# Five instead of four 7-product row pairs in three column pairs of each MLP's first matrix, with the half-width weight blocks in buffers of their own

## The chip, the cores and the metric

The kernel runs on one core of a Trainium2 chip. The metric is the device time of one execution in microseconds (us). Below, TensorE is PE in the profile, VectorE is DVE, ScalarE is ACT, GpSimd is POOL, and SyncE, which issues the weight loads, is SP. A difference of less than 0.2%, some 5 us, is about what a measurement of this kernel cannot tell from no change.

## The reference

A two-layer decoder trunk on 256 tokens of width 2048, in float32: one retention layer with a squared-ReLU MLP, then one latent-attention layer with another such MLP. The change sits in the two MLPs, and the reference for them is short:

```python
def sq_relu_mlp(h, w1, w2):
    return jnp.square(jax.nn.relu(h @ w1)) @ w2
# in each of the two layers, with w1 (2048, 8192) and w2 (8192, 2048):
x = x + sq_relu_mlp(rms_norm(x, norm_mlp[layer]), mlp_w1[layer], mlp_w2[layer])
```

All other parts (the retention projections, the query, key and value projections, the softmax, the rotary tables) stay as they were, apart from where some constants and tables lie in the on-chip memory.

## The kernel before

**Three products for one.** TensorE multiplies operands in a rounded type, so the kernel writes each operand as a high part and a low part. A product of two blocks then takes three matmuls (lines 409 to 411): high by high, high by low, low by high. The high part of a weight block is a cast on ScalarE (line 216, tiles `wh`), the low part is a subtraction on VectorE (line 217, tiles `wl`).

**Quads.** In the MLPs the work comes in quads. A quad is one row pair (256 rows of a weight matrix) by one column pair (1024 columns), that is four weight blocks of 128 rows by 512 columns, loaded by one DMA of 1 MB into a tile `raw`. There are three `raw` buffers. Function `quad` (from line 321) multiplies a quad by the two token tiles in one of two ways:

- **8 products** (24 matmuls): the four blocks are split as they are. ScalarE makes two casts and VectorE two subtractions of 1024 columns.
- **7 products** (21 matmuls), after Strassen and Winograd: VectorE first makes sums of the weight blocks (line 363 with 1024 columns, lines 372 and 373 with 512 each), and then the blocks 11 and 22, the block 21 alone, and two pairs of sums are split. That is three splits of 1024 columns and one of 512, the **half block**. The activations need sums too; `with_sums` (line 451) makes them: three small operations on VectorE, one cast and one subtraction.

**Column pairs.** `gemm_pair` (line 386) runs eight quads, one after the other, over one column pair, and collects the products in PSUM tiles `c11` to `c22`, `p1`, `p5` and `p67`. Its list `kinds` says which row pairs take the 7-product way, so a list such as `SEVEN = (3, 5, 7)` names row pairs. At the end `pair_out` copies six results to SBUF on ScalarE (line 432) and joins them with four operations on VectorE (lines 434 to 439).

**The MLP.** `mlp` (line 864) takes the 8192 hidden columns in four groups of 2048. A group has four column pairs of eight quads each: two of the first matrix (named `u0_2` for layer 0, column pair 2; its quads are `u0_20` to `u0_27`), then two of the second matrix (`d0_10` and `d0_11` for group 1, whose quads are `d0_110` and so on). Column pairs 2, 4 and 6 are the first of the groups 2, 3 and 4. The results of the first matrix are joined (line 448, `summed`), multiplied and clipped on ScalarE (line 877), turned on TensorE (line 235, tiles `hid_tp`), squared and split. The results of the second matrix are added to `x` in device memory by accumulating DMAs from the POOL queue (line 152, tiles `xh`), except in the last group.

**What sets the order.** Every engine works through its own list in order. The lists are made when the program is built: the code issues parts, `later` delays a piece of work by so many quads, and a scheduler then orders each engine's list. At run time an engine waits at the head of its list until what it needs is there. Weight parts `wh` and `wl` have five buffers each. Before the change each of these has 1024 columns, and a half block occupies a whole one:

```python
wh = pool.tile([P, 1024], F32R, tag="wh", bufs=5, name=f"{name}_wh{part}")
wl = pool.tile([P, 1024], F32R, tag="wl", bufs=5, name=f"{name}_wl{part}")
```

A cast can therefore start only when the part five places before it has been multiplied. A new `raw` can be loaded when VectorE and ScalarE have read the quad three places before it.

Of the kernel before, what the change touches and what calls it, by code (L numbers as in the profile page):

```python
# [11 lines left out]
F32 = mybir.dt.float32  # L12
F32R = mybir.dt.float32r
# [3 lines left out]
ALU = mybir.AluOpType  # L17
# [18 lines left out]
P = 128  # L36
NT = 2
S = NT * P
# [7 lines left out]
GROUPS = (4, 4, 4, 4)  # L46
SEVEN, LATE, ODD, HEAD = (3, 5, 7), (5, 7), (1, 3, 5, 7), (2, 4, 6, 7)
QUERY, FOUR = (3, 4, 6, 7), (3, 5, 6, 7)
PI = math.pi

G_MIX0, G_MLP0, G_KV, G_MIX1, G_MLP1 = 0, 16, 32, 48, 64
G_CKV, G_CQ, G_KN, G_QN, G_ALL = 80, 84, 96, 97, 98
C_INVR, C_INVM, C_MASK, C_ID, C_ALL = 0, 128, 160, 544, 672

# [12 lines left out]
def yoco(ctx: ExitStack, tc: tile.TileContext, a):  # L67
    nc = tc.nc
# [6 lines left out]
    def small(w, name):  # L75
        return pool.tile([P, w], F32, tag="small", bufs=36, name=name)

# [19 lines left out]
    def later(n, fn):  # L97
        queue.append((clock[0] + n, next(count), fn))
# [16 lines left out]
    gains = pool.tile([P, G_ALL], F32, name="gains")  # L115
    cst = pool.tile([P, C_ALL], F32, name="cst")
    pos_i = pool.tile([P, NT], I32, name="pos_i")
    gpe = pool.tile([P, 2 * ROPE], F32, name="gpe")
    nc.scalar.dma_start(gains, a["gains"])
    ident = cst[:, C_ID : C_ID + P]  # L120
    mask = cst[:, C_MASK : C_MASK + 3 * P]
    neg_half = pool.tile([P, 16], F32, name="neg_half")
    nc.gpsimd.memset(neg_half, -0.5)
# [114 lines left out]
    def stream(w, chunk, cols, name, use, done=None, before=None):  # L238
# [5 lines left out]
        for half in range(2):  # L244
            wh = pool.tile([P, 1024], F32R, tag="wh", bufs=5, name=f"{name}_wh{half}")
            wl = pool.tile([P, 1024], F32R, tag="wl", bufs=5, name=f"{name}_wl{half}")
            cuts = 1
# [73 lines left out]
    def quad(w, chunk, x, mm, name, split_ends=False):  # L321
# [362 lines left out]
    def start(half):  # L684
        first_inputs(half)
        if half == 4:
            nc.sync.dma_start(pos_i, a["pos"])
            nc.sync.dma_start(cst, a["cst"])
            nc.sync.dma_start(gpe, a["gpe"])
        if half == 5:  # L690
            ret_tables()
        if half == 7:
            for b in range(NB):
                later(2 + b, lambda b=b: load_x(b))
            later(6, scale_tables)
            later(18, lambda: mla_sc.append(sincos(cst[:, C_INVM : C_INVM + 32], 32, "tm")))
            later(26, mla_tables)
# [166 lines left out]
    def mlp(layer, act, r, done):  # L864
        w1, w2 = a[f"mlp_w1_{layer}"], a[f"mlp_w2_{layer}"]
        f0 = 0
        for gi, nf in enumerate(GROUPS):
# [74 lines left out]
    rc, ckv = [], []  # L942
    kpe_t = pool.tile([P, 2, S], F32R, name="kpe_t")

# [167 lines left out]
    def score(b, qt, qpe):  # L1112
# [16 lines left out]
        for t in range(NT):  # L1129
            cols = slice(t * P, t * P + (t + 1) * P)  # L1130
            cut = mask[:, cols].unsqueeze(1).to_broadcast([P, 2, (t + 1) * P])
            nc.vector.tensor_tensor(p[t], sc[:, :, cols], cut, op=ALU.add)
# [82 lines left out]
def _constants():  # L1215
# [9 lines left out]
    causal = np.where(i[None, :] <= i[:, None], 0.0, -1e30)  # L1225
    cst[:, C_MASK : C_MASK + 3 * P] = np.concatenate([causal, np.zeros((P, P)), causal], axis=1)
    cst[:, C_ID : C_ID + P] = np.eye(P)
# [65 lines left out]
```

## Time and profile before

| what | value |
|---|---|
| median of 3 runs (lowest to highest) | 2459.8 us (2458.24 to 2460.84) |
| the profiled execution, its own time | 2458.1 us |
| its span, first to last instruction | 2456.3 us |
| TensorE busy | 2446.2 us, 11614 instructions |
| TensorE weight loads busy | 2057.6 us |
| VectorE busy | 2212.2 us, 2919 instructions |
| ScalarE busy | 1641.3 us |
| GpSimd busy | 238.0 us |
| DMA | 521.05 MB, mean 212 GB/s |

The busy share of TensorE counts matmuls that overlap, each with a modelled end, so it says that TensorE is nearly never idle and not how fast it is. The starts of its instructions tell the pace. VectorE's and ScalarE's idle time stands in the timeline in brackets ahead of what ended it. Outside the span lie 1.8 us of the profiled execution's time.

### The profile page before, as it was taken

What the parts mean: (1) busy time and instruction counts of PE and PEld (TensorE: products, weight loads), DVE (VectorE), ACT (ScalarE), POOL (GpSimd) and SP (SyncE); (2) the same over time, 40 slices, a digit from 0 to 9 for tenths busy, and PEclk for the clock granted to TensorE, in tenths of its full rate; (3) what the DMA queues carried; (4) which work ended last, traced back from release to release, by engine and by line L of the source; (5) the groups of instructions that cost most, each with busy time, mean ns of one, the idle gap of its engine ahead of it and who ended that gap; (6) DMA issues with size and microseconds to landing.
All of it is one profiled execution on the core that took longest, in us unless ns stands there. A gap on an engine that the chain in (4) does not pass through costs nothing.

```text
span 2456.3 us, 31721 instructions
## 1 busy us (share of the span) xinstructions
PE 2446.2 (100%) x11614; PEld 2057.6 (84%) x11614; DVE 2212.2 (90%) x2919; ACT 1641.3 (67%) x2307; POOL 238.0 (10%) x287
## 2 busy tenths in 40 slices
PE   9999999999999999999999999999999999999999
PEld 7888888888888888888888888998888888888887
DVE  7899899888899999999999998777899999999998
ACT  6566666556676767667676777577667667676674
POOL 6400001000000010010110001101000100100100
PEclk9999999999999999999999999999999999999999
DMA  8555569556565586695786555444555865957854
GB/s 309 207 201 191 192 202 259 191 183 224 197 218 194 196 254 218 207 272 187 241 253 213 200 202 180 155 162 173 197 199 205 252 228 194 262 198 229 264 209 170
DMA packets 93692, 521.05 MB, mean 212 GB/s; under 512 B 11104, under 2 KB 12512, under 8 KB 40288
## 3 DMA queue, kind: packets, MB, share of 16 engines
q1 hardware_dynamic: 72144, 472.83, 55.2%
q0 software_dynamic: 21248, 46.15, 8.9%
q8 instruction: 91, 1.49, 0.2%
q14 instruction: 65, 0.53, 0.1%
q10 hardware_dynamic: 144, 0.05, 0.0%
HBM read 479.14 MB, written 39.85 MB: 211 GB/s over the span
## 4 chain that ended last, share of the span: by engine, by line
PE 92%; DVE 2%; ACT 1%; issue 0%; DMA 0%; POOL 0%; ACTq 0%; DVEq 0%
PE u_c L411 7%; PE u_c L410 7%; PE u_c L409 7%; PE d_c L411 6%; PE d_c L410 6%; PE d_c L409 6%; PE rp_c L411 3%; PE rp_c L409 3%; PE rp_c L410 3%; PE u_p L411 2%; PE u_p L410 2%; PE u_p L409 2%; PE rq_acc L307 2%; PE rk_acc L307 2%; PE ro_c L411 2%; PE ro_c L409 2%
## 5 line engine op out<-in xcount | busy, mean ns | idle before, releaser
L217 DVE TENSOR_TENSOR d_wl<-d_raw,d_wh 128x1024 fp32r<-128x1024 f32 (+1 forms) x256 | 278.7, 1111 | 31.6 <-ACT d_wh L216 31.6
L217 DVE TENSOR_TENSOR u_wl<-u_raw,u_wh 128x1024 fp32r<-128x1024 f32 (+1 forms) x256 | 279.3, 1113 | 29.8 <-ACT u_wh L216 29.8
L409 PE MATMUL u_c<-u_wh,n 128*128 128x512 f32 x712 | 278.3, 392 | 0.0
L411 PE MATMUL u_c<-u_wh,n 128*128 128x512 f32 x712 | 277.2, 389 | 0.0
L410 PE MATMUL u_c<-u_wl,n 128*128 128x512 f32 x712 | 277.2, 389 | 0.0
L409 PE MATMUL d_c<-d_wh,hid 128*128 128x512 f32 x706 | 275.4, 392 | 0.5 <-ACT d_wh L216 0.5
L411 PE MATMUL d_c<-d_wh,hid 128*128 128x512 f32 x706 | 275.0, 390 | 0.0
L410 PE MATMUL d_c<-d_wl,hid 128*128 128x512 f32 x706 | 274.8, 389 | 0.0
L216 ACT CAST u_wh<-u_raw 128x1024 fp32r<-128x1024 f32 (+1 forms) x256 | 241.3, 973 | 49.6 <-PE u_c L411 24.1
L216 ACT CAST d_wh<-d_raw 128x1024 fp32r<-128x1024 f32 (+1 forms) x256 | 240.3, 971 | 39.9 <-PE d_c L411 16.6
L216 ACT CAST d_wh<-d_u 128x1024 fp32r<-128x1024 f32 x106 | 108.1, 1051 | 119.7 <-DVE d_u L373 82.6
L216 ACT CAST u_wh<-u_u 128x1024 fp32r<-128x1024 f32 x104 | 106.2, 1052 | 116.0 <-DVE u_u L373 77.3
L411 PEld LDWEIGHTS u_c<-u_wh,n 128*128 128x128 f32 x712 | 133.7, 188 | 27.8
L410 PEld LDWEIGHTS u_c<-u_wl,n 128*128 128x128 f32 x712 | 133.8, 188 | 27.4 <-DVE u_wl L217 0.3
L409 PEld LDWEIGHTS u_c<-u_wh,n 128*128 128x128 f32 x712 | 133.7, 188 | 27.0
L409 PEld LDWEIGHTS d_c<-d_wh,hid 128*128 128x128 f32 x706 | 132.6, 188 | 28.2 <-ACT d_wh L216 1.4
L411 PEld LDWEIGHTS d_c<-d_wh,hid 128*128 128x128 f32 x706 | 132.5, 188 | 27.6
L410 PEld LDWEIGHTS d_c<-d_wl,hid 128*128 128x128 f32 x706 | 132.6, 188 | 27.5 <-DVE d_wl L217 0.4
L216 ACT CAST rp_wh<-rp_raw 128x1024 fp32r<-128x1024 f32 x112 | 103.8, 945 | 74.2 <-PE rp_c L411 49.2
L217 DVE TENSOR_TENSOR rp_wl<-rp_raw,rp_wh 128x1024 fp32r<-128x1024 f32 x112 | 119.7, 1090 | 16.4 <-ACT rp_wh L216 16.2
L217 DVE TENSOR_TENSOR u_wl<-u_u,u_wh 128x1024 fp32r<-128x1024 f32 x104 | 123.5, 1222 | 3.1 <-ACT u_wh L216 2.8
L217 DVE TENSOR_TENSOR d_wl<-d_u,d_wh 128x1024 fp32r<-128x1024 f32 x106 | 125.8, 1221 | 0.0
(570 smaller groups left out, 6505.3 us busy)
## 6 DMA issues: line engine op xcount, KB each, us to landing
u_raw<-in_mlp_w SPq DMA_DIRECT2D x128, 1024.0 KB, 5.4
d_raw<-in_mlp_w SPq DMA_DIRECT2D x128, 1024.0 KB, 4.9
rp_raw<-in_ret_w_gv SPq DMA_DIRECT2D x56, 1024.0 KB, 4.8
ro_raw<-in_ret_w_out SPq DMA_DIRECT2D x32, 1024.0 KB, 4.9
uq_raw<-in_mla_w_uq SPq DMA_DIRECT2D x24, 768.0 KB, 4.3
rq_raw<-in_ret_w_qk SPq DMA_DIRECT2D x16, 1024.0 KB, 4.9
rk_raw<-in_ret_w_qk SPq DMA_DIRECT2D x16, 1024.0 KB, 4.8
xh<-d_c POOLq DMA_DIRECT2D x48, 256.0 KB, 6.1
```

The costliest lines, as they stand in the source:

```text
L216: nc.scalar.copy(h, src)
L217: return nc.vector.tensor_tensor(l, src, h.bitcast(F32), op=ALU.subtract)
L307: nc.tensor.matmul(acc[f], wh[:, cols], a.rearrange("p i s -> p (i s)"), start=k == 0, stop=k == nk - 1)
L409: nc.tensor.matmul(dst, ah, bh, start=n == 0, stop=False)
L410: nc.tensor.matmul(dst, ah, bl, start=False, stop=False)
L411: nc.tensor.matmul(dst, al, bh, start=False, stop=n == total[key] - 1)
```

## The change

In column pairs 2, 4 and 6 of both layers the list `ODD = (1, 3, 5, 7)` becomes `FIVE = (1, 3, 5, 6, 7)`, and the quads are taken in the order 0, 1, 3, 2, 5, 4, 6, 7. Row pair 6 of the activations has no sums, so `sum_again` makes them anew in each of the first three groups, four quads into that group's last column pair. For this, half blocks get tags of their own (`wh1`, `wl1`, one buffer each, 512 columns), so that the five buffers (`wh2`, `wl2`) hold only whole parts. Room for it comes from smaller constants, from fewer small tiles, and from tables that share a slot or are loaded when they are needed.

```diff
+FIVE = (1, 3, 5, 6, 7)
...
-        return pool.tile([P, w], F32, tag="small", bufs=36, name=name)
+        return pool.tile([P, w], F32, tag="small", bufs=26, name=name)
...
-            wh = pool.tile([P, 1024], F32R, tag="wh", bufs=5, name=f"{name}_wh{part}")
-            wl = pool.tile([P, 1024], F32R, tag="wl", bufs=5, name=f"{name}_wl{part}")
+            wh, wl = (
+                pool.tile([P, n * 512], F32R, tag=f"{i}{n}", bufs=5 if n == 2 else 1, name=f"{name}_{i}{part}")
+                for i in ("wh", "wl")
+            )
...
-    rope_tab = pool.tile([P, 2, S], F32, name="rope_tab")
-    pe_tabs = [[pool.tile([P, 2, ROPE], F32, name=f"petab{t}{i}") for i in range(2)] for t in range(NT)]
+    rope_tab = pool.tile([P, 2, S], F32, tag="tab", bufs=2, name="rope_tab")
+    pe_tab = pool.tile([P, NT, 2, 2, ROPE], F32, tag="tab", bufs=2, name="pe_tab")
...
+    def inverse(lo, n, name):
+        inv = f2k([n], name)
+        nc.sync.dma_start(inv, a["cst"][:, lo : lo + n])
+        return inv
+
     def mla_tables():
+        gpe = f2k([2 * ROPE], "gpe")
+        nc.sync.dma_start(gpe, a["gpe"])
...
-        ret_sc.append(sincos(cst[:, C_INVR : C_INVR + 128], 128, "tr"))
+        ret_sc.append(sincos(inverse(C_INVR, 128, "invr"), 128, "tr"))
...
-            nc.sync.dma_start(cst, a["cst"])
-            nc.sync.dma_start(gpe, a["gpe"])
+            nc.sync.dma_start(cst, a["cst"][:, C_MASK:])
...
+        def sum_again(name):
+            v = act[6][0]
+            u = f2k([2, S], f"{name}_u")
+            nc.vector.tensor_tensor(u, v[:, :, 0].bitcast(F32), v[:, :, 1].bitcast(F32), op=ALU.add)
+            again[:] = [*act[:6], (v, with_sums(u, name)), act[7]]
...
-                seven = SEVEN if p % 2 else ODD if p else LATE
+                seven = SEVEN if p % 2 else FIVE if p else LATE
                 gemm_pair(
-                    w1, p * 8, act, [i in seven for i in range(8)], f"u{layer}_{p}", lambda c, p=p, up=up: up(c, p)
+                    w1, p * 8, again if p % 2 == 0 and p else act, [i in seven for i in range(8)], f"u{layer}_{p}",
+                    lambda c, p=p, up=up: up(c, p), order=(0, 1, 3, 2, 5, 4, 6, 7) if seven is FIVE else None,
                 )
...
+                if p and not last:
+                    later(4, lambda gi=gi: sum_again(f"n{layer}{gi}"))
+
```

The change moves instructions at many places, since the scheduler orders the lists anew. Two of them matter most. The first is ScalarE's list where the column pair `d0_01` ends and `u0_20`, the first quad of the changed column pair, begins. The `d0_01` tiles are the results that `pair_out` copies. Before:

```order
L216 CAST d0_017_wh3_8105<-d0_017_u0_8073 128x1024
L432 COPY d0_01_c22_8115<-d0_01_c22_7805 128x512
L216 CAST u0_20_wh0_8134<-u0_20_raw_8132 128x1024
L432 COPY d0_01_c12_8117<-d0_01_c12_7801 128x512
L216 CAST u0_20_wh1_8154<-u0_20_raw_8132 128x1024
L432 COPY d0_01_c11_8119<-d0_01_c11_7793 128x512
```

And with the change:

```order
L216 CAST d0_017_wh3_8115<-d0_017_u0_8083 128x1024
L216 CAST u0_20_wh0_8144<-u0_20_raw_8142 128x1024
L434 COPY d0_01_c22_8125<-d0_01_c22_7806 128x512
L216 CAST u0_20_wh1_8164<-u0_20_raw_8142 128x1024
L434 COPY d0_01_c12_8127<-d0_01_c12_7802 128x512
L216 CAST u0_21_wh0_8190<-u0_21_raw_8183 128x1024
L434 COPY d0_01_c11_8129<-d0_01_c11_7794 128x512
```

Each of the casts `u0_20_wh0`, `u0_20_wh1` and `u0_21_wh0` has moved ahead of a copy that waits for TensorE. The same happens where `d0_01` itself begins, and at most other column pairs.

The second place is VectorE's list at the end of the changed column pair and into the next one (`u0_30`, `u0_31`). The `u0_2` tiles are its joined results. Before:

```order
L217 TENSOR_TENSOR u0_27_wl3_8451<-u0_27_u0_8418,u0_27_wh3_8450 128x1024
L217 TENSOR_TENSOR u0_30_wl0_8480<-u0_30_raw_8477,u0_30_wh0_8479 128x1024
L217 TENSOR_TENSOR u0_30_wl1_8500<-u0_30_raw_8477,u0_30_wh1_8499 128x1024
L448 TENSOR_TENSOR u0_2_c11_8464<-u0_2_c11_8464,u0_2_p1_8468 128x512
L434 TENSOR_TENSOR u0_2_v_8472<-u0_2_p67_8205,u0_2_p1_8468 128x512
L435 TENSOR_TENSOR u0_2_u_8473<-u0_2_p67_8205,u0_2_v_8472 128x512
L217 TENSOR_TENSOR u0_31_wl0_8555<-u0_31_raw_8552,u0_31_wh0_8554 128x1024
L438 TENSOR_TENSOR u0_2_v_8472<-u0_2_p5_8470,u0_2_v_8472 128x512
L448 TENSOR_TENSOR u0_2_c21_8466<-u0_2_c21_8466,u0_2_u_8473 128x512
```

And with the change:

```order
L217 TENSOR_TENSOR u0_27_wl3_8471<-u0_27_u0_8438,u0_27_wh3_8470 128x1024
L217 TENSOR_TENSOR u0_30_wl0_8500<-u0_30_raw_8497,u0_30_wh0_8499 128x1024
L217 TENSOR_TENSOR u0_30_wl1_8520<-u0_30_raw_8497,u0_30_wh1_8519 128x1024
L217 TENSOR_TENSOR u0_31_wl0_8575<-u0_31_raw_8572,u0_31_wh0_8574 128x1024
L450 TENSOR_TENSOR u0_2_c11_8484<-u0_2_c11_8484,u0_2_p1_8488 128x512
L436 TENSOR_TENSOR u0_2_v_8492<-u0_2_p67_8215,u0_2_p1_8488 128x512
L437 TENSOR_TENSOR u0_2_u_8493<-u0_2_p67_8215,u0_2_v_8492 128x512
L217 TENSOR_TENSOR u0_31_wl1_8591<-u0_31_raw_8572,u0_31_wh1_8590 128x1024
L440 TENSOR_TENSOR u0_2_v_8492<-u0_2_p5_8490,u0_2_v_8492 128x512
L450 TENSOR_TENSOR u0_2_c21_8486<-u0_2_c21_8486,u0_2_u_8493 128x512
```

One more split of 1024 columns, `u0_31_wl0`, now stands ahead of the joins that end in `u0_2_c21`, and `u0_31_wl1` has taken its place among them.

More of the change, by code (lines that the diff above doesn't have):

```diff
@@ L52 @@
 G_CKV, G_CQ, G_KN, G_QN, G_ALL = 80, 84, 96, 97, 98
-C_INVR, C_INVM, C_MASK, C_ID, C_ALL = 0, 128, 160, 544, 672
+C_INVR, C_INVM, C_MASK, C_ID, C_ALL = 0, 128, 160, 416, 544
 MAGIC = 1.5 * 2.0**23
@@ L115, in yoco @@
     gains = pool.tile([P, G_ALL], F32, name="gains")
-    cst = pool.tile([P, C_ALL], F32, name="cst")
+    cst = pool.tile([P, C_ALL - C_MASK], F32, name="cst")
     pos_i = pool.tile([P, NT], I32, name="pos_i")
-    gpe = pool.tile([P, 2 * ROPE], F32, name="gpe")
     nc.scalar.dma_start(gains, a["gains"])
-    ident = cst[:, C_ID : C_ID + P]
-    mask = cst[:, C_MASK : C_MASK + 3 * P]
-    neg_half = pool.tile([P, 16], F32, name="neg_half")
+    mask = cst[:, 0 : 2 * P]
+    ident = cst[:, 2 * P : 3 * P]
+    neg_half = pool.tile([P, 8], F32, name="neg_half")
     nc.gpsimd.memset(neg_half, -0.5)
@@ L244, in stream @@
         for half in range(2):
-            wh = pool.tile([P, 1024], F32R, tag="wh", bufs=5, name=f"{name}_wh{half}")
-            wl = pool.tile([P, 1024], F32R, tag="wl", bufs=5, name=f"{name}_wl{half}")
+            wh = pool.tile([P, 1024], F32R, tag="wh2", bufs=5, name=f"{name}_wh{half}")
+            wl = pool.tile([P, 1024], F32R, tag="wl2", bufs=5, name=f"{name}_wl{half}")
             cuts = 1
@@ L606, in yoco @@
     scale = (NOPE + ROPE) ** -0.5
-    rope_tab = pool.tile([P, 2, S], F32, name="rope_tab")
-    pe_tabs = [[pool.tile([P, 2, ROPE], F32, name=f"petab{t}{i}") for i in range(2)] for t in range(NT)]
+    rope_tab = pool.tile([P, 2, S], F32, tag="tab", bufs=2, name="rope_tab")
+    pe_tab = pool.tile([P, NT, 2, 2, ROPE], F32, tag="tab", bufs=2, name="pe_tab")
+    pe_tabs = [[pe_tab[:, t, i] for i in range(2)] for t in range(NT)]
     gqn = pool.tile([P, 1], F32, name="gqn")
+    def inverse(lo, n, name):
+        inv = f2k([n], name)
+        nc.sync.dma_start(inv, a["cst"][:, lo : lo + n])
+        return inv
     def mla_tables():
+        gpe = f2k([2 * ROPE], "gpe")
+        nc.sync.dma_start(gpe, a["gpe"])
         sm = mla_sc[0](no_turn[0])
@@ L695, in start @@
             later(6, scale_tables)
-            later(18, lambda: mla_sc.append(sincos(cst[:, C_INVM : C_INVM + 32], 32, "tm")))
+            later(18, lambda: mla_sc.append(sincos(inverse(C_INVM, 32, "invm"), 32, "tm")))
             later(26, mla_tables)
@@ L865, in mlp @@
         w1, w2 = a[f"mlp_w1_{layer}"], a[f"mlp_w2_{layer}"]
+        again = []
+        def sum_again(name):
[3 more added lines that the diff above has]
+            again[:] = [*act[:6], (v, with_sums(u, name)), act[7]]
         f0 = 0
@@ L942, in yoco @@
     rc, ckv = [], []
-    kpe_t = pool.tile([P, 2, S], F32R, name="kpe_t")
+    kpe_t = pool.tile([P, 2, S], F32R, tag="tab", bufs=2, name="kpe_t")
     def downed(acc, b):
@@ L1130, in score @@
             cols = slice(t * P, t * P + (t + 1) * P)
-            cut = mask[:, cols].unsqueeze(1).to_broadcast([P, 2, (t + 1) * P])
+            cut = mask[:, P - t * P : 2 * P].unsqueeze(1).to_broadcast([P, 2, (t + 1) * P])
             nc.vector.tensor_tensor(p[t], sc[:, :, cols], cut, op=ALU.add)
@@ L1225, in _constants @@
     causal = np.where(i[None, :] <= i[:, None], 0.0, -1e30)
-    cst[:, C_MASK : C_MASK + 3 * P] = np.concatenate([causal, np.zeros((P, P)), causal], axis=1)
+    cst[:, C_MASK : C_MASK + 2 * P] = np.concatenate([np.zeros((P, P)), causal], axis=1)
     cst[:, C_ID : C_ID + P] = np.eye(P)
```

## The prediction

> **What bounds the kernel now.** I read the page's totals first, then the chain that ended last, then the timelines of TensorE and VectorE around the first changed column pair (u0_2, about 892 to 934 us). The totals and the costliest group of matmuls:
>
> ```profile
> span 2456.3 us, 31721 instructions
> PE 2446.2 (100%) x11614; PEld 2057.6 (84%) x11614; DVE 2212.2 (90%) x2919; ACT 1641.3 (67%) x2307; POOL 238.0 (10%) x287
> ...
> L409 PE MATMUL u_c<-u_wh,n 128*128 128x512 f32 x712 | 278.3, 392 | 0.0
> ```
>
> TensorE is busy for 2446.2 of 2456.3 us, so at most 10.1 us of the span are not TensorE's, and in the MLP groups it waits for nothing (the 0.0 at the row's end). The chain of waits shows the same by its regularity; these are the first transposes after two column pairs that stand one group apart:
>
> ```profile
> 770.95 0.87 PE hid_tp L235 x8
> ...
> 939.11 0.87 PE hid_tp L235 x8
> ```
>
> A group takes 168.16 us. The mean of 392 ns is not what a matmul costs, because each starts before the one ahead of it ends. The timeline of TensorE gives the pace:
>
> ```profile
> 894.75 0.39 PE L409 MATMUL u_c<-u_wh,n 128*128 128x512 f32 x1
> ...
> 895.43 0.39 PE L409 MATMUL u_c<-u_wh,n 128*128 128x512 f32 x1
> ```
>
> Between these two starts lie three matmuls, one product: **0.68 us a product, 0.227 a matmul**. By the mean of 392 ns a product would seem to cost 1.18.
>
> [...]
>
> VectorE is second, at 90%. How near it is to TensorE shows where the split of a part ends shortly before TensorE wants it, in the second quad of the column pair:
>
> ```profile
> 898.47 2.36 DVE L217 TENSOR_TENSOR u_wl<-u_u,u_wh 128x1024 fp32r<-128x1024 f32 x2
> ...
> 900.41 0.39 PE L410 MATMUL u_c<-u_wl,n 128*128 128x512 f32 x1
> ```
>
> The first of these two splits ends at 898.47 + 1.22 = 899.69, and the first matmul that reads it starts at 900.41: 0.72 us of lead. So a slower VectorE is felt at once, and the question is whether its added work fits.
>
> **What the change removes.** In each of six column pairs (u0_2, u0_4, u0_6, u1_2, u1_4, u1_6) one 8-product quad becomes a 7-product quad: three matmuls, 0.68 us. The order of TensorE's list has 18 rows fewer, and nothing else on it is new. 6 x 0.68 = **4.1 us**, if nothing comes to wait.
>
> **What it adds on VectorE.** The rows of one 8-product quad (the first) and one 7-product quad (the next five), closed by the start of the quad after:
>
> ```profile
> 900.74 2.36 DVE L217 TENSOR_TENSOR u_wl<-u_raw,u_wh 128x1024 fp32r<-128x1024 f32 x2
> 903.01 1.22 DVE L363 TENSOR_TENSOR u_u<-u_raw 128x1024 f32<-128x1024 f32 x1
> 904.27 0.69 DVE L372 TENSOR_TENSOR u_u<-u_u,u_raw 128x512 f32<-128x512 f32 x1
> 904.99 0.69 DVE L373 TENSOR_TENSOR u_u<-u_u,u_raw 128x512 f32<-128x512 f32 x1
> 905.60 1.82 DVE L217 TENSOR_TENSOR u_wl<-u_raw,u_wh 128x1024 fp32r<-128x1024 f32 x2
> 907.34 2.36 DVE L217 TENSOR_TENSOR u_wl<-u_u,u_wh 128x1024 fp32r<-128x1024 f32 x2
> 909.68 1.23 DVE L217 TENSOR_TENSOR u_wl<-u_raw,u_wh 128x1024 fp32r<-128x1024 f32 x1
> ```
>
> By starts, the 8-product quad takes 903.01 - 900.74 = 2.27 us and the 7-product one 909.68 - 903.01 = 6.67. TensorE takes 24 x 0.227 = 5.4 and 21 x 0.227 = 4.8 for them, so each 7-product quad costs VectorE lead and each 8-product quad gives some back. The conversion adds 6.67 - 2.27 = 4.40 us per column pair.
>
> The new `sum_again` has five operations on VectorE: one of 512 columns, one of 256, two of 128, and a split of 512. Rows of the same kinds:
>
> ```profile
> 947.17 0.42 DVE L455 TENSOR_TENSOR hid_sum<-hid_u 128x256 f32<-128x256 f32 x1
> 947.50 0.69 DVE L373 TENSOR_TENSOR u_u<-u_u,u_raw 128x512 f32<-128x512 f32 x1
> ...
> 950.65 0.29 DVE L457 TENSOR_TENSOR hid_sum<-hid_u,hid_sum 128x128 f32<-128x128 f32 x1
> 950.85 0.69 DVE L217 TENSOR_TENSOR u_wl<-u_raw,u_wh 128x512 fp32r<-128x512 f32 x1
> 951.45 1.23 DVE L217 TENSOR_TENSOR u_wl<-u_u,u_wh 128x1024 fp32r<-128x1024 f32 x1
> ```
>
> By starts again: 0.33 for 256 columns, 0.20 for 128, 0.60 for 512. 0.60 + 0.33 + 2 x 0.20 + 0.60 = 1.93 us, in the column pair ahead of each changed one. A third cost lies in the order: the sums of a quad now mostly stand one behind the other. Line 372 then starts 904.27 - 903.01 = 1.26 us after line 363, where a 1024-column operation is otherwise followed after 1.13, and line 373 starts 0.72 after line 372, not 0.60. Three quads that had other work between their sums lose it, at four places by 0.12 or 0.13, which makes 0.5 us. Finally TensorE arrives 0.68 us sooner at the end. **Together 4.40 + 1.93 + 0.5 + 0.68 = 7.5 us** that VectorE must find between the start of d0_01 and the end of u0_2.
>
> **What it has there.** VectorE's idle time in that stretch, from its timeline:
>
> ```profile
> 848.91 1.23 DVE L217 TENSOR_TENSOR d_wl<-d_raw,d_wh 128x1024 fp32r<-128x1024 f32 x1 [1.77 <-ACT d_wh L216]
> ...
> 871.70 1.23 DVE L363 TENSOR_TENSOR d_u<-d_raw 128x1024 f32<-128x1024 f32 x1 [1.60 <-DMA d_raw<-in_mlp_w]
> ...
> 889.72 1.23 DVE L217 TENSOR_TENSOR u_wl<-u_raw,u_wh 128x1024 fp32r<-128x1024 f32 x1 [1.57 <-ACT u_wh L216]
> ...
> 912.91 1.23 DVE L363 TENSOR_TENSOR u_u<-u_raw 128x1024 f32<-128x1024 f32 x1 [2.01 <-DMA u_raw<-in_mlp_w]
> ...
> 930.51 1.23 DVE L217 TENSOR_TENSOR u_wl<-u_raw,u_wh 128x1024 fp32r<-128x1024 f32 x1 [1.16 <-ACT u_wh L216]
> 931.95 1.23 DVE L217 TENSOR_TENSOR u_wl<-u_raw,u_wh 128x1024 fp32r<-128x1024 f32 x1 [0.21 <-ACT u_wh L216]
> 933.41 0.69 DVE L448 TENSOR_TENSOR u_c<-u_c,u_p 128x512 f32<-128x512 f32 x1 [0.23 <-ACT u_p L432]
> ```
>
> Without the first row that is 1.60 + 1.57 + 2.01 + 1.16 + 0.21 + 0.23 = 6.8 us. The first 1.77 comes on top, 8.55 in all, if d0_01 starts sooner. That is the point of the first order shown above: the first casts of a column pair stood behind a copy that waits for TensorE, and now stand ahead of it, so VectorE need not wait for them. The half blocks' own buffers allow it, because a whole part now takes the buffer of the fifth whole part before it.
>
> So VectorE is between 0.7 us short (none of the 1.77 used) and 1.0 us ahead (all of it used) at each of the six places. Short means that TensorE waits at the end, where the second order stands:
>
> ```profile
> 937.08 0.69 DVE L448 TENSOR_TENSOR u_c<-u_c,u_u 128x512 f32<-128x512 f32 x1
> ...
> 938.13 2.21 ACT L877 ACTIVATE u_c<-u_c,n_r 128x512 f32<-128x512 f32 x3
> ...
> 938.95 1.04 PE L235 MATMUL hid_tp<-cst,u_c 128*128 128x128 f32 x8
> ```
>
> The first of the three clippings ends about 938.9, and the transposes that read it start then: this place has 0.2 us to spare at most. The middle of the two ends lies at +0.15, just enough; some of the six will fall short. I take 0.1 us of wait at each: **6 x 0.1 = 0.6 us**.
>
> **What I cost at nothing.** ScalarE's added casts (1.5 parts of 1024 columns and one of 512) fit, at 67% busy; without that cover they would cost as much as VectorE's. The half block's single buffer makes its cast wait for the same block of the quad before. That is multiplied 9 x 0.227 = 2.0 us into its quad, and the next half is needed at 4.8 + 1.6 = 6.4, so 4.4 us remain for a cast and a split of 0.6 each. The table constants move to later loads, and the rows that bear on them are these:
>
> ```profile
> 59.55 0.73 POOL L206 TENSOR_TENSOR n_r<-n_m,neg_half 128x2 f32<-128x2 f32 x1 [1.89 <-DVE n_m L205]
> ...
> 170.84 0.38 SPq L727 DMA_DIRECT2D dec<-in_decay  x1
> ...
> 177.79 0.19 DVE L620 SCALAR_TENSOR_TENSOR petab<-tm_sc,gpe 128x32 f32<-128x32 f32 x1
> ```
> ```profile
> dec<-in_decay SPq DMA_DIRECT2D x8, 128.0 KB, 4.9
> ```
>
> GpSimd's first table chain has 1.89 us to spare for a later start. The load of `gpe` now stands on SP one load away from the `dec` load that was issued at 170.84; with 4.9 us to land it is there near 176, and it is read at 177.79. If it came late, VectorE would lose 1 to 3 us once. The smaller ring of small tiles and the shared table slot wait for readers long done, so I take 0 (bounds 0 and 1 us).
>
> **The sum.** -4.1 + 0.6 = -3.5 us. The profiled execution took 2458.1 and would take 2454.6; it was 1.7 us below the median of its runs, so against the median of 2459.8 I forecast **2456.3 us**.
>
> **The rivals.**
>
> *VectorE takes the saving back.* If none of the 1.77 us is used, each place is 0.7 us short, 6 x 0.7 = 4.2 us against 4.1: about 2459.9. For it: the lead of 0.72 us and the split that now stands ahead of the joins. Against it: the casts that moved.
>
> *The waits for loads stay.* The 1.60 and 2.01 us were waits for `raw`. If the second stays as it is, since a load still lands late beside the accumulating DMAs, VectorE is short by 0.7 + 2.0 = 2.7 us at each place: 6 x (2.7 - 0.68) = 12 us, about **2472, slower**. It decides from 1.5 us of wait a place, where 6 x (1.5 - 0.68) passes 4.9. Against it: VectorE comes later to these loads, so the same landing is no longer waited for.
>
> *More than the matmuls.* Casts ahead of copies everywhere, and buffers that hold more, could remove some of the 10.1 us that are not TensorE's. 1 to 2 us of these with the full 4.1 give about 2454.
>
> *VectorE's full durations.* If each operation held VectorE for its whole duration (1.22 for 1024 columns, 0.69 for 512), a 7-product quad would take 4 x 1.22 + 3 x 0.69 = 6.95 and an 8-product one 2.44. With four joins of 0.69 the changed column pair needs 5 x 6.95 + 3 x 2.44 + 2.76 = 44.8 against TensorE's 177 x 0.227 = 40.2, and six places lose some 25 us: about 2485. Against it: the starts, which lie 1.13 and 0.60 apart. [...]
>
> **How the numbers follow.** The forecast, 2454.9 to 2458.5, has 0.55. The saving taken back, 2458.5 to 2462, has 0.20. More than the matmuls, under 2454.9, has 0.15. The two slower cases, 2464.7 and above, have 0.10 together, 0.08 of it the loads. The range runs from 2454.0 to 2462.0: it takes in both ends of VectorE's shortfall and the once-lost 1 to 3 us, and leaves out the slower cases and the far end of the gain. Differences below 0.2% (4.9 us) are about what a measurement of this kernel cannot tell from none. 4.1 us is 0.17%, so the saving alone stays inside: faster 0.15, same 0.75, slower 0.10.
>
> **What would show it.** Group periods of 168.16 - 0.68 = 167.5 us with VectorE's waits at the six places nearly gone would show the forecast right. TensorE waiting for `hid_tp` by 0.5 us or more in groups 2 to 4 would show the saving taken back; TensorE waiting for a `wl` after a DVE wait for `u_raw` would show the slower case. A matmul pace other than 0.227 would make the sum wrong from its first term.

## The result, and the profile after

| | before | changed |
|---|---|---|
| median of six runs, us | 2459.8 (2458.2 to 2462.7) | 2471.3 (2469.4 to 2478.6) |
| ratio to before, 95% interval | | 1.0051 [1.0041, 1.0061] |
| profiled execution, us; its span | 2458.1; 2456.3 | 2469.4; 2467.6 |
| matmuls | 11614 | 11596 |

The change cost 11.5 us where 3.5 were forecast as a gain, so the prediction was wrong, and its range (up to 2462.0) missed too. The totals of the changed kernel show the 18 matmuls gone and the span longer by 11.3 us:

```profile
span 2467.6 us, 31736 instructions
...
PE 2445.4 (99%) x11596; PEld 2056.2 (83%) x11596; DVE 2254.3 (91%) x2979; ACT 1641.2 (67%) x2325; POOL 245.1 (10%) x287
```

The waits of TensorE in the changed kernel (us in total, times, the longest) name the place. In the list of before there is no row for `hid_tp`; its longest wait, 1.2 us, stands at the program's start.

```profile
PE hid_tp L235 <- ACT u_c L894: 11.8, 6, 3.8
```

Six waits, and six changed column pairs: they are the transposes of u0_2, u0_4, u0_6, u1_2, u1_4 and u1_6. (Single waits below are counted from start to start of TensorE's rows, less the usual distance; by that count the six are 12.8 us.) The starts of the first transposes of each column pair, from TensorE's timeline, separate gain and loss (distance between neighbours, us):

| from, to | before | changed |
|---|---|---|
| u0_1 to u0_2; u0_3 to u0_4; u0_5 to u0_6 | 124.88 each | 124.20; 124.20; 124.19 |
| u0_2 to u0_3; u0_4 to u0_5; u0_6 to u0_7 | 43.28 each | 44.89; 44.99; 48.85 |
| u1_2 to u1_3; u1_4 to u1_5; u1_6 to u1_7 | 43.28 each | 45.00; 44.14; 48.16 |

The 0.68 us of each place arrive in full (in the second layer the distances are 124.25, 124.20 and 124.20), and the stretch behind gives back 16.4 us in all. The chain of waits of the changed kernel shows what stands there, at the first place (start, us, what ran):

```profile
931.35 1.23 DVE u_wl L217
932.59 6.87 DMA u_raw<-in_mlp_w
939.48 0.34 ACT u_wh L216
939.82 0.18 issue
940.00 0.73 ACT u_c L894
940.73 0.04 issue
940.77 0.98 PE hid_tp L235 x7
```

Read from below: seven transposes waited for a clipping (L894), the clipping for a cast (L216), the cast for a load of 6.87 us, and the load for VectorE to free its buffer. ScalarE's timeline has the same three rows with the idle time before them:

```profile
935.48 2.23 ACT L216 CAST u_wh<-u_raw 128x1024 fp32r<-128x1024 f32 x2
939.48 0.62 ACT L216 CAST u_wh<-u_raw 128x512 fp32r<-128x512 f32 x1 [1.77 <-DMA u_raw<-in_mlp_w]
940.00 1.95 ACT L894 ACTIVATE u_c<-u_c,n_r 128x512 f32<-128x512 f32 x3
```

The 512-column cast is that of a half block. ScalarE's list has it just ahead of the three clippings (the numbers at the ends of the names are left out):

```
before:  CAST u0_32_wh0   CAST u0_32_wh1                      ACTIVATE u0_2_c21   u0_2_c12   u0_2_c22
changed: CAST u0_32_wh0   CAST u0_32_wh1   CAST u0_33_wh1     ACTIVATE u0_2_c21   u0_2_c12   u0_2_c22
```

The load took longer in company. Before, the last two loads were issued 6.1 us apart (927.11 and 933.20) and the second landed at 937.98; now they are 3.4 us apart (929.18 and 932.59), since VectorE frees the buffer of the last quad later, and the second landed at 939.46. The rows by stretch (busy us of TensorE, its weight loads, VectorE, ScalarE and GpSimd, then the granted clock, the share of the DMA engines and GB/s), of before:

```profile
933.00:938.00 5.00, 5.00 (x23) 4.14 (x23) 4.73 (x8) 5.00 (x7) 0.00 (x0) 1.00 0.72 232
```

and of the changed kernel:

```profile
933.00:940.00 7.00, 6.41 (x29) 5.02 (x27) 6.96 (x11) 5.11 (x8) 0.00 (x0) 1.00 0.94 302
```

The DMA engines are busy for 0.94 of the stretch in which the load is waited for, against 0.72. The first place is not all six, though. The two loads stand 3.4 us apart at every place, 6.1 to 6.7 before. But at the third and the sixth place, where loads of `x` run too, the same load took 7.51 and 7.80 us already before, and at the fifth it took 6.1 us before and after. That cost nothing before, since the half cast stood behind the clippings then.

With a buffer of its own, the half block of u0_33 no longer waits for a whole part's buffer, so the scheduler could put its cast early (without the own buffers it does not stand there, as experiment 3 shows); the load that it reads had not landed. It stands there at the end of all 16 column pairs of the first matrices, and only at the six changed ones does it wait. VectorE, on which the prediction dwelt, was not late. Its timeline in the changed kernel:

```profile
937.28 0.68 DVE L450 TENSOR_TENSOR u_c<-u_c,u_u 128x512 f32<-128x512 f32 x1
```

The join that the clipping of `c21` needs ended at 937.96, and the clipping started at 940.00. Before, the join ended at 937.77; but the changed kernel runs 0.86 us later there (the first transposes of u0_1 start at 814.93 and 814.07), so by the distance from them the join comes 0.67 us sooner, as TensorE does.

### The profile page after: what moved, and what is told of

Its sections match the earlier page's. It is cut to its first block, busy times and chain, and to the rows that moved or that the text cites. A ratio compares the mean times of both kernels' runs of the same rounds, so it can differ in the third digit from the quotient of the medians.

```text
span 2467.6 us, 31736 instructions
## 1 busy us (share of the span) xinstructions
PE 2445.4 (99%) x11596; PEld 2056.2 (83%) x11596; DVE 2254.3 (91%) x2979; ACT 1641.2 (67%) x2325; POOL 245.1 (10%) x287
## 4 chain that ended last, share of the span: by engine, by line
PE 83%; DVE 11%; DMA 2%; issue 2%; ACT 1%; POOL 0%; SPq 0%; ACTq 0%; DVEq 0%
PE d_c L413 7%; PE d_c L411 7%; PE d_c L412 7%; DVE u_wl L217 5%; PE u_c L411 4%; PE u_c L413 4%; PE u_c L412 4%; PE rp_c L411 3%; PE rp_c L413 3%; PE rp_c L412 3%; PE rq_acc L307 2%; PE rk_acc L307 2%; PE d_p L412 2%; PE d_p L411 2%; PE d_p L413 2%; DMA u_raw<-in_mlp_w 2%
## 5 line engine op out<-in xcount | busy, mean ns | idle before, releaser
L216 ACT CAST u_wh<-u_raw 128x1024 fp32r<-128x1024 f32 (+1 forms) x256 | 239.8, 957 | 81.9 <-PE u_c L413 43.1
L217 DVE TENSOR_TENSOR u_wl<-u_raw,u_wh 128x1024 fp32r<-128x1024 f32 (+1 forms) x256 | 273.4, 1097 | 11.6 <-ACT u_wh L216 11.4
L216 ACT CAST d_wh<-d_raw 128x1024 fp32r<-128x1024 f32 (+1 forms) x256 | 242.0, 967 | 59.2 <-PE d_c L413 43.7
L411 PE MATMUL u_c<-u_wh,n 128*128 128x512 f32 x676 | 266.0, 394 | 0.0
L413 PE MATMUL u_c<-u_wh,n 128*128 128x512 f32 x676 | 264.0, 391 | 0.0
L412 PE MATMUL u_c<-u_wl,n 128*128 128x512 f32 x676 | 263.7, 390 | 0.0
L216 ACT CAST u_wh<-u_u 128x1024 fp32r<-128x1024 f32 x116 | 117.2, 1056 | 91.1 <-DVE u_u L375 78.6
L216 ACT CAST d_wh<-d_u 128x1024 fp32r<-128x1024 f32 x106 | 106.9, 1057 | 93.9 <-DVE d_u L375 93.9
L216 ACT CAST rp_wh<-rp_raw 128x1024 fp32r<-128x1024 f32 (+1 forms) x112 | 104.0, 944 | 77.0 <-PE rp_c L413 54.9
L413 PEld LDWEIGHTS u_c<-u_wh,n 128*128 128x128 f32 x676 | 127.3, 188 | 26.9
L412 PEld LDWEIGHTS u_c<-u_wl,n 128*128 128x128 f32 x676 | 127.7, 189 | 25.9
L411 PEld LDWEIGHTS u_c<-u_wh,n 128*128 128x128 f32 x676 | 127.6, 189 | 25.8
L217 DVE TENSOR_TENSOR u_wl<-u_u,u_wh 128x1024 fp32r<-128x1024 f32 x116 | 138.2, 1217 | 1.2 <-ACT u_wh L216 0.9
L217 DVE TENSOR_TENSOR rp_wl<-rp_raw,rp_wh 128x1024 fp32r<-128x1024 f32 (+1 forms) x112 | 120.6, 1092 | 10.9 <-ACT rp_wh L216 10.4
```

The costliest lines, as they stand in the source:

```text
L216: nc.scalar.copy(h, src)
L217: return nc.vector.tensor_tensor(l, src, h.bitcast(F32), op=ALU.subtract)
L411: nc.tensor.matmul(dst, ah, bh, start=n == 0, stop=False)
L412: nc.tensor.matmul(dst, ah, bl, start=False, stop=False)
L413: nc.tensor.matmul(dst, al, bh, start=False, stop=n == total[key] - 1)
```

## The experiments

**Theory A**: two things together cost the time: the half cast's place on ScalarE's list ahead of the clippings, and a load that VectorE's added work makes late. **Theory B**: VectorE's added work is the bound by itself, and the wait would only move elsewhere. **Theory C**: the place on the list is enough. Each kernel has its median beside its own runs of before (2459.7 for the first four, 2460.2, 2460.1 and 2460.4 for the later groups), and a ratio with its 95% interval.

**1. The half cast behind the clippings (e1_clip_first).** `clipped[0]` holds the last clipping that was written out, and `halved` is `split` that returns both operations. (In kernels with added code the line numbers are 5 to 14 higher.)

```diff
-            low = low_part[0] = split(wh[:, : n * 512], wl[:, : n * 512], src)
+            high, low = halved(wh[:, : n * 512], wl[:, : n * 512], src)
+            low_part[0] = low
+            if n == 1 and clipped[0] is not None:
+                queued_behind(high, clipped[0])
```

> The changed kernel, with one dependency more: the cast of a half block is put on ScalarE's list behind the last clipping of the column pair before, wherever it stood ahead of it. Nothing that is computed changes. Theory A (ScalarE's list): in the six changed places the cast of the next pair's first half block stands ahead of three clippings and waits 1.0 to 4.2 us for its load; the clippings, the transposes and TensorE wait with it. Taken out, the six waits for hid_tp (12.8 us) and the slow matmuls behind the two longest (2.7 us) go, and the time is 2471.3 - 15.5 = 2455.8, say 2455 to 2458; the waits for hid_tp fall under 0.3 us each. Theory B (VectorE's added work): the load is late because VectorE frees its buffers late, and VectorE itself is at its limit; then the wait only moves, from hid_tp to a wh or wl of the next pair, and the time stays above 2465.

Measured: 2457.2 us (2456.0 to 2460.3), ratio 0.9991 [0.9982, 1.0000]. One dependency gives back 14 us. The waits for `hid_tp` in this kernel:

```profile
PE hid_tp L240 <- ACT u_c L902: 0.5, 1, 0.5
```

All eight transposes of u0_2 run in one piece, and the distances of the table above are 124.20 and 43.34 at the first place. (Theory A had all waits under 0.3 us; one of 0.5 is left.) The load still takes 5.7 us at the first place, and no clipping waits for it. A is borne out, and B is out as the bound of the changed kernel.

**2. The buffers alone (e2_buffers_alone).** `FIVE` becomes `ODD` again, and `sum_again` goes.

```diff
-                seven = SEVEN if p % 2 else FIVE if p else LATE
+                seven = SEVEN if p % 2 else ODD if p else LATE
```

> The buffers, the tables and the rings of the changed kernel, without the fifth 7-product quad, its order and the sums of the seventh block. The cast of a half block still stands ahead of the three clippings at all 16 column pairs of the first matrices. Theory A, which needs both the place on the list and a late load: in the kernel before, the load in question landed at 937.98 and the clipping began at 938.13, so the cast (0.62 us) costs at most 0.5 us at a place, and the time is 2459 to 2462. Theory C (the place on the list is enough): the six waits appear here too, 2470 or more. Theory B (VectorE's added work alone): no difference from before, 2459.8 within 2 us.

Measured: 2461.0 us (2459.0 to 2463.0), ratio 1.0004 [0.9995, 1.0012]. The half cast stands ahead of the clippings at all 16 column pairs, and the row for `hid_tp` is

```profile
PE hid_tp L235 <- ACT u_c L894: 0.4, 2, 0.3
```

The place alone costs 0.4 us of waits, at the third and the sixth place, where the load took 6.3 and 6.4 us: C is out.

**3. The fifth quad without the buffers (e3_product_alone).** All parts share five whole buffers again.

```diff
-                pool.tile([P, n * 512], F32R, tag=f"{i}{n}", bufs=5 if n == 2 else 1, name=f"{name}_{i}{part}")
+                pool.tile([P, 1024], F32R, tag=f"{i}2", bufs=5, name=f"{name}_{i}{part}")
```

> The changed kernel, with half blocks and whole parts in one ring of five buffers again, as before; the fifth 7-product quad, its order and the sums of the seventh block stay. On ScalarE's list no half cast then stands ahead of the clippings. Theory A: the six waits go with it; the saving of 4.1 us is there less what VectorE lacks when the casts stand behind the copies again (0 to 0.7 us a place): 2455 to 2460. Theory B: VectorE has 2.4 us of work more in each changed pair than TensorE has time and the waits stay: 2465 to 2472.

Measured: 2470.5 us (2468.6 to 2472.5), ratio 1.0041 [1.0027, 1.0055]. The time is that of B, and A's number for this kernel is missed, but the waits are others than in the changed kernel. TensorE waits for parts that are not ready, for `wh` inside the changed pairs and for `wl` mostly in the pairs behind them:

```profile
PE u_c L411 <- ACT u_wh L216: 6.3, 6, 1.4
PE u_p L412 <- DVE u_wl L217: 2.9, 6, 1.0
```

The `wh` casts themselves wait for VectorE. This is the one behind the first of the six waits (906.95 us):

```profile
905.85 2.00 ACT L216 CAST u_wh<-u_u 128x1024 fp32r<-128x1024 f32 x2 [3.19 <-DVE u_u L375]
```

And VectorE's timeline has the idle row at the start of u0_2 again that the prediction quoted with 1.57 us, because the first casts stand behind the copies again:

```profile
892.04 1.23 DVE L217 TENSOR_TENSOR u_wl<-u_raw,u_wh 128x1024 fp32r<-128x1024 f32 x1 [1.45 <-ACT u_wh L216]
```

So the own buffers are what makes room for the fifth quad on VectorE, and they are also what let the half cast go where it does harm.

**4. An 8-product quad between the last two 7-product ones (e4_order_swapped).**

```diff
-order=(0, 1, 3, 2, 5, 4, 6, 7) if seven is FIVE else None
+order=(0, 1, 3, 2, 5, 6, 4, 7) if seven is FIVE else None
```

> The changed kernel with two quads of the changed pairs changed over: the last four run as 5, 6, 4, 7 in place of 5, 4, 6, 7, so an 8-product quad stands between the last two 7-product ones. The half cast still stands ahead of the clippings. Theory A with a late load as the second half of the cause: VectorE has read the quad before the last sooner, the loads of the next pair are issued further apart, and the cast waits less: 2457 to 2464. Theory C (the place on the list alone): 2471, as the changed kernel. Theory B: VectorE has the same work in all, so 2468 to 2471.

Measured: 2475.7 us (2470.8 to 2479.8), ratio 1.0061 [1.0048, 1.0075]: a miss for A's number. `hid_tp` was waited for by 12.6 us, and the load at the first place took 7.42 us. The two loads were now issued 4.54 us apart in place of 3.41, and the waits did not fall. So the two 7-product quads in a row are not needed for a late load; what a distance of 6 us, as before, would have done was not tried.

**5. How much room VectorE has (e5_one_more_sum).** On top of e1, the first sum of quad 6 is written twice, with the same values.

> The kernel e1_clip_first with one VectorE operation more in each of the six changed column pairs: the 1024-column sum of the last 8-to-7 quad is made twice (1.13 us from start to start). It asks how much room VectorE has left there. If VectorE has no room (theory B), each place loses up to 1.13 us: 2457.2 + 6.8 = 2464. If it has more than 1.1 us in hand, as the idle rows of the changed kernel say (0.57 + 0.27 + 0.32 + 0.91 us between 845 and 945 us), it costs nothing: 2457 to 2459.

Measured: 2462.3 us (2459.8 to 2464.2), ratio 1.0007 [0.9999, 1.0016]. This is neither of the two cases. Of 6 x 1.13 = 6.8 us, 5.1 arrive by the medians and 4.6 by the distances between first transposes in the two traces, some 0.8 a place: VectorE has 0.3 to 0.4 us in hand at a place. The idle rows that made 1.1 us and more of it were no measure.

**6. The same in the odd column pairs (e6_odd_too).** On top of e1, `again` is used and quad 6 is a 7-product one in u*_3, u*_5 and u*_7 as well.

> The kernel e1_clip_first with the sixth block's sums used in the odd column pairs as well: u*_3, u*_5 and u*_7 get a fourth 7-product quad (3, 5, 6, 7). Another 18 matmuls go, 4.1 us; VectorE and ScalarE get the work of six more conversions (4.4 us each on VectorE) in stretches where they also make the hidden blocks. If there is room in the odd pairs: 2457.2 - 4.1 = 2453. If VectorE has none: each place loses the 4.4 + 0.68 us less what idle time there is, 2457 to 2475; the likeliest is a loss, about 2465.

Measured: 2476.5 us (2475.4 to 2478.7), ratio 1.0068 [1.0056, 1.0080]. That is above the range. TensorE waits 3.5 us for `wl` and 3.5 for `wh` parts, in the odd pairs and the changed ones behind them, so there is no room for the work. The 7.5 us for `hid_tp` have another cause: 3.1 and 3.8 us of start-to-start distance stand at the third and the sixth place, and the chain there is that of the changed kernel over again. The dependency of e1 holds back half casts only; here the cast of a whole part stands ahead of the three clippings and waits for its load:

```profile
1282.85 1.04 ACT L225 CAST u_wh<-u_raw 128x1024 fp32r<-128x1024 f32 x1 [4.03 <-DMA u_raw<-in_mlp_w]
```

So the run does not tell what the odd pairs alone would have cost.

**7 and 11. The loads of x at the third and the sixth place (e7_x_later, e11_x_held).** In both, on the changed kernel, these loads come later; first by three quads, then by a dependency.

```diff
-            later(2 * b, lambda b=b: bring(b))
+            later(2 * b + wait, lambda b=b: bring(b))
...
+                if after:
+                    tc.add_manual_dep(ins.ins, after[0].ins.name, ...)
```

> The changed kernel with the half cast left ahead of the clippings, and only the loads of x for the last group of each layer moved three quads later. In the third and the sixth changed place four of these loads stand between the load that the half cast waits for and the one before it; it takes 9.31 and 8.55 us there, and 6.1 to 7.0 at the other four places. If it is the company of these loads that makes the third and sixth place worse, their waits fall from 3.97 and 3.21 us to about 1.6, and the slow matmuls behind them go: 2471.3 - 4.0 - 2.7 = 2464.6, say 2463 to 2467. If not, 2471 as before.

> The changed kernel, half cast ahead of the clippings, with the loads of x for the last group held back by a dependency on a split in the fifth quad of the last column pair, some 20 us later. In e7_x_later two of the four loads still stood at the third place (1271.1 and 1271.7 us), and its load took 8.58 us. If the company of the x loads makes the third and sixth places worse, the load there takes 6 to 7 us as at the other four, the waits fall from 3.97 and 3.21 us to 1 to 2, and the slow matmuls behind them go: 2465 to 2468. If not, the load stays near 8.5 us and the time at 2471.

Measured: 2471.8 us, ratio 1.0043 [1.0031, 1.0055], and 2471.6 us, 1.0044 [1.0032, 1.0056]. In the first, two of the four loads still stood there. In the second all were gone; the rows by stretch, first of the changed kernel, then of e11_x_held:

```profile
1270.00:1280.00 10.00, 7.68 (x35) 6.07 (x33) 9.96 (x13) 5.86 (x9) 1.90 (x4) 1.00 1.03 376
```
```profile
1271.00:1281.60 10.60, 9.46 (x43) 7.53 (x41) 10.56 (x15) 8.35 (x12) 0.86 (x1) 1.00 0.86 276
```

The load at the third place took 7.16 us in place of 9.31, and the wait fell from 3.97 to 2.64 us; at the sixth from 3.21 to 1.99. But at the fourth place, where no x load ever stood, the load took 8.26 us in that run and the wait was 3.77. So the company of the x loads explains about 1.3 us at each of two places, and the landing scatters by as much from run to run. The time did not fall. In the profiled execution of e11_x_held, 3.2 us of waits for `wl` parts (`u_p`, two of them) stand beside the 10.3 us for `hid_tp`; the changed kernel had none of 0.2 us or more, and where they come from was not followed.

**8. The table's constants sooner (e8_clip_invm).** On top of e1:

```diff
+            later(10, lambda: invm.append(inverse(C_INVM, 32, "invm")))
-            later(18, lambda: mla_sc.append(sincos(inverse(C_INVM, 32, "invm"), 32, "tm")))
+            later(18, lambda: mla_sc.append(sincos(invm[0], 32, "tm")))
```

> The kernel e1_clip_first with the load of the second table's frequencies (32 columns) issued eight quads sooner. In the changed kernel GpSimd waits 21.6 us for it and makes its table from 122 to 150 us in place of 101 to 121, beside VectorE work of which 1024 columns then take 1.3 to 1.5 us, not 1.22; TensorE waits 0.5 us at 139.7 and 1.1 to 1.9 at 172 to 174. If the late table is the reason, the chain is back at 101 to 121, both waits fall under 0.3 us, and the time is 2457.2 - 1.3 to - 2.0, so 2455.2 to 2455.9. If these waits have another reason (the order of the loads of gpe and dec), 2457.2 stays.

Measured: 2456.2 us (2454.6 to 2458.0), ratio 0.9983 [0.9975, 0.9992], 0.17% faster than before, and faster than the change as made. GpSimd's first row of the table, and the mean of four of VectorE's 1024-column splits between 122 and 151 us, in the changed kernel:

```profile
122.33 4.03 POOL L572 TENSOR_SCALAR tm_ang<-invm,pos_f 128x32 f32<-128x32 f32 x2 [21.63 <-DMA invm<-in_cst]
```
```profile
L217 DVE TENSOR_TENSOR rq_wl<-rq_raw,rq_wh 128x1024 fp32r<-128x1024 f32 x4 | 5.5, 1388 | 0.0
```

and in e8_clip_invm:

```profile
101.64 0.72 POOL L580 TENSOR_SCALAR tm_ang<-invm,pos_f 128x32 f32<-128x32 f32 x2
```
```profile
L217 DVE TENSOR_TENSOR rq_wl<-rq_raw,rq_wh 128x1024 fp32r<-128x1024 f32 x4 | 4.8, 1214 | 0.0
```

The chain is back at 101 us, these splits are back at 1.21 us, the wait of 0.5 us at 139.7 is gone, and that near 172 is 0.28 us (e1: 1.85). The 1.0 us between the two medians is less than their scatter; that the waits went is shown by the trace.

**9 and 10. VectorE's work without the products (e9_buffers_more_sums, e10_more_sums_clip).** On e2, the sums are written more than once, with the same values; e10 has the dependency of e1 too.

```diff
+        if name[:4] in ("u0_2", "u0_4", "u0_6", "u1_2", "u1_4", "u1_6"):
+            for _ in range(2 if name[4:] == "7" else 1):
+                nc.vector.tensor_tensor(u[0], ...)
```

> The kernel e2_buffers_alone (buffers and tables of the change, half cast ahead of the clippings, products as before) with five sums of 1024 columns made a second time in each of the six column pairs: one in quads 1, 3 and 5, two in quad 7. That is 5 x 1.13 = 5.65 us more on VectorE per pair, about what the conversion puts there (4.40 + 0.5 + 0.68 = 5.6), and no matmul less. Theory A with both parts (place on the list and a load made late by VectorE's work, whatever the work is): waits for hid_tp of 1 to 4 us come back at the six places, with ScalarE idle for the load ahead of the half cast; 2461.0 + 8 to 15 = 2469 to 2476. If it takes the 7-product quad itself (its place in the order, its sums of the seventh block): 2461 to 2464, since 5.65 us fit the 6.8 us of idle time there.

> The kernel e9_buffers_more_sums with the half cast behind the clippings. Theory A: whatever e9 loses by the half cast's wait goes: 2459 to 2463, and the waits for hid_tp fall under 0.4 us. If VectorE's extra work is itself what TensorE waits for: as e9.

Measured: e9 2477.0 us (2471.3 to 2483.5), 1.0069 [1.0057, 1.0081]; e10 2464.0 (2461.8 to 2466.2), 1.0017 [1.0008, 1.0025]. The waits of e9, and ScalarE's timeline at its first place:

```profile
PE hid_tp L235 <- ACT u_c L900: 14.9, 6, 3.5
```
```profile
944.54 0.62 ACT L216 CAST u_wh<-u_raw 128x512 fp32r<-128x512 f32 x1 [1.98 <-DMA u_raw<-in_mlp_w]
```

And the waits of e10:

```profile
PE hid_tp L240 <- ACT u_c L908: 2.3, 6, 1.2
```

The picture of the changed kernel comes back without a fifth 7-product quad, from VectorE's work and the place on the list together, and the dependency takes 13 us of it away. Both end 1 us above their ranges. In e10 the clippings wait for VectorE's joins, so VectorE itself is short there, by some 0.4 us a place. Side by side, in us:

| | half cast ahead | half cast behind |
|---|---|---|
| products as before | 2461.0 (e2) | not run without the sooner constants |
| 5.65 us more on VectorE a pair | 2477.0 (e9) | 2464.0 (e10) |
| fifth 7-product quad | 2471.3 (the change) | 2457.2 (e1) |

**12. What the fifth quad is worth alone (e12_mended_no_product).** e8 with the edits of e2.

> The kernel e8_clip_invm (half cast behind the clippings, frequencies loaded sooner) without the fifth 7-product quad, its order and the sums of the seventh block. It asks what the product conversion alone is worth once nothing is in its way. If all 18 matmuls arrive at the end: 2456.2 + 4.1 = 2460.3, say 2459.5 to 2461. If VectorE takes a part of them back in e8_clip_invm (there TensorE waited 2.1 us for wl parts at 1072 to 1101 and 0.7 us for hid_tp): 2457.5 to 2459.

Measured: 2458.3 us (2456.9 to 2458.9), ratio 0.9990 [0.9981, 0.9999]. The difference to e8 is 2.1 us, half of 4.1. In the profiled execution of e8 TensorE waited 1.4 us for `u_wl` parts and 0.5 for `hid_tp`, as the second case says; both ratios are uncertain by about 2 us. The traces tell more. From the first transposes of u0_1 to those of u0_7, and of u1_1 to u1_7, e1's profiled execution is 3.3 us shorter than e12's, but e8's only 0.5: at its second place a load took 10.4 us, VectorE stood idle for it by 1.68 us (at 1088.27), and 2.8 us of TensorE's waits follow. That execution of e8 is the slowest of its eleven. So 3.3 of the 4.1 us can arrive, and a late load can take most of it back; how often it does stays open.

## Why the prediction was wrong

- **18 matmuls, -4.1 us: right.** Every changed pair ends 0.68 us sooner, in the changed kernel as well (124.88 to 124.20). (That TensorE waits for nothing in the groups is not quite so: before, it waited 0.5 us for `d_wh` parts at the end of the second layer's last group. The sum does not use it.)
- **VectorE 0.7 short to 1.0 ahead, 0.1 us of wait a place: right.** Of the 8.55 us of idle time 1.16 are left in the changed kernel's trace (0.57 + 0.27 + 0.32), so some 7.4 were used, of 7.5 counted. The join of `c21` kept up with TensorE, e5 measures 0.3 to 0.4 us of room, and in e1's trace 0.8 of the 4.1 us are lost, 0.13 a place. That the casts ahead of the copies give the 1.77 us is shown by e3, which does without: the row is back with 1.76, and TensorE waits 9.2 us for parts.
- **"ScalarE's added casts ... fit, at 67% busy": this step failed.** The sum of ScalarE's work did fit. What was not asked is where on its list the new casts stand, and what each waits for. The excerpts shown with the change were of ScalarE's list at the start of the changed pair and of VectorE's at its end; the one row that mattered was on ScalarE's list at the end. It was priced at 0 and cost 11.8 us of waits, and the slow matmuls behind the two longest.
- **The half block's single buffer, at nothing: right for the wait looked at** (4.4 us of margin), and blind to the reverse: a buffer that is free early lets its cast be queued early, ahead of work that is urgent.
- **The table constants, at nothing: wrong by 1 to 2 us.** The working treated `gpe` and GpSimd's first chain. The second table's frequencies, `invm`, were now issued at 117.7 us, and GpSimd waited 21.6 us for them.
- **The rivals.** "The waits for loads stay" gave about 2472 and 0.08, close to the 2471.3 measured, but by another mechanism: VectorE was to wait for `raw`; it was ScalarE that did. VectorE's wait of 2.01 us is gone in the changed kernel and that of 1.60 is down to 0.57. That the numbers agree is chance. "VectorE takes the saving back" is what e3 shows, larger than priced: it takes back the 4.1 us and 10.8 more, 2.5 a place, where 0.7 a place was priced. The price counted the 1.57 us as time that VectorE could use; in e3 1.45 of it stay idle beside the 1.76, which makes VectorE 2.2 us short.
- **The sign to look for was ambiguous.** A wait for `hid_tp` of 0.5 us or more was to show VectorE too slow. The wait came, with VectorE on time. The releaser of a wait has to be followed one step further, to what it waited for itself.

With the half cast's place and the table constants mended, e8 ran at 2456.2 us, where the forecast was 2456.3; by e12 that is a gain from the buffers as much as from the products, so it is not the forecast's sum come true, and that the two numbers agree is luck.

## What to carry to other kernels

An engine that works its list in order is not made safe by being 67% busy (ScalarE here, whose half casts ahead of the clippings cost TensorE 11.8 us of waits): for each instruction that a change adds or frees to move, ask what it waits for, and what stands behind it. A tile that gets its own buffer loses a wait, and that wait may have been what kept its writer behind more urgent work; look at the list behind every wait for a DMA. Where a scheduler decides, one dependency that keeps such an instruction behind the urgent ones (here 14 us) is cheaper than taking the change back. It has to hold every instruction of the kind: in e6 the cast of a whole part did what that of the half block had done.

## What the runs showed of the hardware

**The clock after a wait.** Behind the two longest waits of the changed kernel, the third of 3.97 us and the sixth of 3.21, the clock granted to TensorE was 0.50 of the full one (from 1281.4 to 1284.6 us, and from 2339.4 to 2342.6). The rows by stretch of the changed kernel, behind the third wait:

```profile
1281.50:1285.50 4.00, 4.00 (x15) 3.50 (x16) 1.52 (x3) 3.86 (x7) 0.00 (x0) 0.60 0.63 254
1285.50:1290.00 4.50, 4.50 (x25) 3.76 (x24) 4.47 (x8) 1.02 (x3) 0.24 (x1) 1.00 0.00 0
```

The granted clock was 0.60 on the mean of the first stretch, and while it was down matmuls started 0.43 us apart (1283.46, 1283.88 and 1284.31 us), not 0.227. Behind the other four waits, of 0.8 to 1.7 us, it was 1.00 (940 to 946, 1109 to 1115, 1999 to 2005 and 2167 to 2174 us). In e9 it was 0.72 from 945 to 951 and 0.53 from 1289.5 to 1295.5 us, behind the waits at the first and the third place, and 1.00 from 2181 to 2186, behind that at the fifth. At the third place of e11_x_held, behind a wait of 2.64 us, matmuls started 0.23 us apart from 1283.92 us on. How long a wait has to be for a slow stretch to follow is not shown. The third wait of the changed kernel, of 3.97 us, cost 5.6 with the slow stretch behind it (48.85 - 43.28).

**VectorE beside GpSimd.** Four splits of 1024 columns took 1388 ns on the mean in the changed kernel, where GpSimd's table ran at the same time, and 1214 in e8_clip_invm, where it did not, 14% more. A split grew by 0.17 us on the mean, beside operations of GpSimd of 0.5 to 1.4 us. GpSimd's first two operations of the table took 4.03 us together in the changed kernel (from 122.33 us) and 0.72 before (from 100.91 us). VectorE worked beside them both times (before in rows at 100.95 and 101.62 us, of 0.75 us each), so the runs do not show what made them longer.

**Loads in company.** A load of 1 MB took 4.8 us alone (issued at 940.73, before; from 940.7 to 945.6 us 1.06 MB were moved in all); the one that the half cast waited for took 5.6 to 9.6 us where others overlapped it (a DMA share of 0.86 to 1.03 in the stretches shown above). The same load at the same place varied by up to 1.6 us between the changed kernel, e7 and e11, at the four places without loads of `x`.
